# More seven-product steps in the early blocks of a hybrid decoder layer

## The chip, the cores and the metric

The kernel runs on one core of a Trainium2 chip. The metric is the device time of one execution in microseconds (us), lower is better. Before the change three runs gave 1722.56, 1724.4 and 1725.03 us; the median is 1724.4 us.

The engines of a core that matter here: TensorE multiplies (PE in the profile, its weight loads PEld), VectorE (DVE) and ScalarE (ACT) work elementwise, SyncE (SP) issues most DMA transfers. Each engine works through its own list of instructions in the order of the program, and waits on semaphores where another engine must be done first.

## What is computed

One layer of a decoder with two parallel branches, for 256 positions and 2048 channels in float32. The part that the change touches is the first large projection, `a @ W_in`, where `a` is the normalised input and `W_in` has 17408 columns that are shared out among attention, recurrence and gates:

```python
a = rmsnorm(h, norm_mix_pre[layer])
proj = a @ w_in[layer]
q_a, k_a, v_a, q_r, f_r, i_r, g_r, gate_a, gate_r = split_columns(proj)
...
y = jax.nn.sigmoid(gate_a) * (attn @ w_attn_branch[layer]) + jax.nn.sigmoid(gate_r) * (r_out @ w_hgrn_branch[layer])
h = h + rmsnorm(y @ w_mix_out[layer], norm_mix_post[layer])
a = rmsnorm(h, norm_ffn_pre[layer])
gt, up = jnp.split(a @ w_ffn_gate_up[layer], [D_FF], axis=-1)
ff = (jax.nn.silu(gt) * up) @ w_ffn_down[layer]
h = h + rmsnorm(ff, norm_ffn_post[layer])
```

## The kernel before

**Precision.** Every float32 operand is split into a rounded high part and a remainder, low = value - high. A product of two float32 tiles is three matmuls: high x high, high x low, low x high. The split of the weights is made on the chip as they stream in: ScalarE rounds (the high part), VectorE subtracts (the low part).

**Blocks and steps.** The program is a list of blocks, each a product of the activations with some columns of a weight matrix, and each block is a list of steps. The early stage of the kernel is two narrow blocks (1024 columns of the recurrence's output gate in all, line 1286), and then eight wide blocks of 1024 columns each: four for the two branch gates, three for the attention values, one for the recurrence's values (the list `early`, line 1289). After those come other stages, which the change leaves alone.

**A wide block** (class `Wide`) has eight steps. Step (m, s) takes the m-th 256 rows of the weights in two halves k = 0, 1 of 128 rows, and the block's two groups of 512 columns g = 0, 1: four weight tiles of 128 x 512. The activations are likewise two halves k by two sides of 128 positions. So a step is a 2 x 2 block product.

- s = 0, a **plain step**: eight products, 24 matmuls. Its split is one activation of 128 x 2048 (line 328) and one subtraction of 128 x 2048 (line 330).
- s = 1, a **seven-product step**: the scheme of Strassen in Winograd's form, seven products, 21 matmuls. Its split first forms sums of weight tiles on VectorE (line 334, 128 x 1024; lines 340 and 341, 128 x 512 each), rounds these on ScalarE (lines 339 and 342), rounds three of the plain tiles on ScalarE (line 345, `dh`), and subtracts for the low parts on VectorE (line 346, 128 x 2048, and line 348, 128 x 1536, `dl`). It needs four sums of activation tiles as well, made once for each m and kept in `x7[m]` (`pair_sums` and `seven_sums`, lines 400 to 422, lines 418, 405, 408 to 411 in the profile).

Of the seven products four go to banks of their own in PSUM (`p1`, `p5`, `p6`, `p7`); after the last seven-product step of a block `gather` (line 389) combines them in one activation and four additions. The outputs of a block are four more banks. `evac_kept` (line 662) ends a block: four additions (line 669), four activations (line 673) and four DMAs to DRAM that ScalarE issues (line 674). The roles of the two pools of four banks, `aux` and `acc`, are exchanged from one block to the next (`flip`).

**Order.** The order of work is written out by hand in the main loop (line 1343). At step n it does, in this order: the split of step n + 2 (`AHEAD` = 2), the load of the weights three further units on, the matmuls of step n, `gather` if this was the block's last seven-product step, some small work from side lanes, and at the end of a block its output. So the splits of the first two steps of a block are issued ahead of the output of the block before. The weight buffer `raw`, the high part `w` and the low part `wl` have three buffers each; the sums (`sum`), `dh` and `dl` of a seven-product step have one each.

**What the steps of the blocks are** stands in two lists (line 37 on). `FIRST`, for the first wide block, has plain steps alone. `EIGHT`, for the other seven (and for the blocks of the feed-forward part), has seven-product steps at its third, fifth and seventh place, with m = 0, 1, 2. The activation sums for `X7` = (0, 1, 2) are made beside the second narrow block, in a side lane (`more_x`, line 643).

Of the kernel before, what the change touches and what calls it, by code (L numbers as in the profile page):

```python
# [32 lines left out]
COL_QR, COL_FR, COL_IR, COL_GR = 9216, 10240, 11264, 12288  # L33
COL_GA, COL_GB = 13312, 15360

X7 = H7 = (0, 1, 2)
FIRST = [(m, 0) for m in range(8)]
EIGHT = [(3, 0), (4, 0), (0, 1), (5, 0), (1, 1), (6, 0), (2, 1), (7, 0)]
DOWN = [[(m, m in by7) for m in range(KF // 2)] for by7 in (range(4, 20, 3), range(3, 19, 3))]

# [50 lines left out]
def tile_hybrid_block(ctx: ExitStack, tc: tile.TileContext, t, out):  # L91
# [18 lines left out]
    def rslot(s):  # L110
        return rpool.tile([P, 1024], F32R, tag="r", bufs=16, name=nm(s))
# [107 lines left out]
    def add_seven(*args, flip, **kw):  # L219
        b = Wide(*args, **kw)  # L220
        b.flip = flip
        blocks.append(b)
        for i in range(b.steps):
            seq.append(Step(b, i, len(units), 0))
            units.append([seq[-1]])
# [187 lines left out]
    def pair_sums(x, which, store, slot):  # L413

        for m in which:
            f = ptile("f").rearrange("p (k t) -> p k t", k=2)
            xs = x.slots[m]
            nc.vector.tensor_add(f, xs[:, :, 0, :].bitcast(F32), xs[:, :, 1, :].bitcast(F32))
            dst = slot().rearrange("p (z n t) -> p z n t", z=2, n=4)
            yield  # L420
            seven_sums(f, dst)()
            store[m] = sums_of(dst)
            yield
# [127 lines left out]
    def flush(q):  # L551
        while q:
            advance(q)
# [6 lines left out]
    xT = Split("xT", KD)  # L560
# [80 lines left out]
    x7 = {}  # L641

    def more_x(c):
        if c + 2 < KD // 2:
            transpose_in(xt, colg, xT, c + 2)
        else:
            lanes[1].append(pair_sums(xT, X7[c - 6 :: 2], x7, lambda: rslot("so")))

# [13 lines left out]
    def evac_kept(key, fn):  # L662
        def go(b):
            dst = keep(key, 1024)
            for s, g in ((0, 0), (0, 1), (1, 0), (1, 1)):
                src = b.bank[s, g]
                if b.rest:
                    e = b.rest[s, g]
                    nc.vector.tensor_add(e, src, e)
                    src = e  # L670
                else:
                    e = eslot()
                nc.scalar.activation(e, src, fn, scale=r1c[:, s : s + 1])
                nc.scalar.dma_start(dst[:, s, g * 512 : (g + 1) * 512], e)
            yield
        return go
# [594 lines left out]
    w_in = t["w_in"][0]  # L1271
# [18 lines left out]
             (COL_GA + 1024, ("a", 1), AF.Sigmoid), (COL_GB + 1024, ("r", 1), AF.Sigmoid)]  # L1290
    early += [(COL_V + 1024 * g, ("v", g), AF.Copy) for g in range(3)] + [(COL_IR, "i", AF.Copy)]
    for n, (col, key, fn) in enumerate(early):
        add_seven(w_in, (col, col + 512), EIGHT if n else FIRST, xT, lambda m: x7[m],
                  evac_kept(key, fn), flip=n % 2 == 1, turn=1,
                  pre=(lambda: flush(lanes[1])) if n == 1 else None)
    for half in range(2):
# [141 lines left out]
```

## Time and profile before

| | |
|---|---|
| median of three runs | 1724.4 us |
| the profiled execution | 1723.16 us |
| its span, first to last instruction | 1721.4 us |
| granted TensorE clock, mean | 0.998 |
| first wide block on TensorE | 62.5 to 106.1 us |
| the seven other early wide blocks | 106.1 to 396.4 us |
| bytes moved by DMA | 344.78 MB |

How the profile is read: times are microseconds from the span's start. A line of the timeline has the start, the duration, the engine, the line of the program, the operation, the tile written and the tiles read, and in square brackets how long the engine had been idle before and which instruction of which engine ended that. A line of the chain has start, duration, engine, tile, line and the number of instructions. A line of a table by stretches has the length, then busy time and number of instructions for PE, PEld, DVE, ACT and POOL, then the granted clock, the busy share of the DMA engines and what they moved in GB/s.

### The profile page before, as it was taken

The numbers are of one execution on the slowest core, as the hardware profiler recorded it, in microseconds if no ns is written. First come the engines' busy times: TensorE is split into PE (matmuls) and PEld (weight loads), VectorE is DVE, ScalarE is ACT, GpSimd is POOL, SyncE is SP. The second block draws the span as 40 slices with busy tenths as digits, with TensorE's granted clock in tenths as the row PEclk, the third lists the DMA queues.
The fourth block names the chain that finished last, engine by engine and source line by source line (L and its number), as shares of the span: only waits on it lengthen the run. The fifth ranks groups of instructions, "written<-read, shape, count | busy, mean of one in ns | idle before, by whom it ended". The sixth has DMA issues, their size and how long they took to land.

```text
span 1721.4 us, 21535 instructions
## 1 busy us (share of the span) xinstructions
PE 1705.4 (99%) x8357; PEld 1431.0 (83%) x8357; DVE 1356.9 (79%) x1477; ACT 895.9 (52%) x1007; POOL 21.7 (1%) x38
## 2 busy tenths in 40 slices
PE   9999999999999999999999999999999999999997
PEld 7788888888888898888888877888888888888886
DVE  6668888886677887777666578888888888898998
ACT  6545555554435434544444465555555555665663
POOL 0000000000000000000000000000000000000000
PEclk9999999999999999999999999999999999999999
DMA  7765666667544645565556745555555555666653
GB/s 253 272 220 208 232 231 221 220 226 251 185 158 159 220 159 172 173 206 167 164 172 202 245 163 196 196 195 196 197 201 201 203 201 201 217 198 217 201 197 116
DMA packets 208742, 344.78 MB, mean 200 GB/s; under 512 B 10960, under 2 KB 77696, under 8 KB 208640
## 3 DMA queue, kind: packets, MB, share of 16 engines
q1 hardware_dynamic: 198848, 319.41, 55.1%
q10 hardware_dynamic: 6880, 13.51, 2.1%
q0 software_dynamic: 2912, 10.49, 1.8%
q8 instruction: 65, 1.06, 0.2%
q14 instruction: 37, 0.30, 0.1%
HBM read 331.83 MB, written 11.53 MB: 199 GB/s over the span
## 4 chain that ended last, share of the span: by engine, by line
PE 96%; DVE 1%; ACT 1%; DMA 1%; issue 0%; SPq 0%; DVEq 0%; ACTq 0%
PE acc L132 62%; PE aux L132 33%; PE aux L491 0%; DVE w L294 0%; PE aux L817 0%; DMA gpost<-in_norm_mix_post 0%; PE acc L1131 0%; DVE fz L1258 0%; ACT w L293 0%; PE aux L1131 0%; PE aux L479 0%; ACT junk L1212 0%; DVE e L1208 0%; ACT junk L1105 0%; DVE wl L330 0%
## 5 line engine op out<-in xcount | busy, mean ns | idle before, releaser
L294 DVE TENSOR_TENSOR w<-raw,w 128x1024 fp32r<-128x1024 f32 (+1 forms) x225 | 274.1, 1219 | 188.0 <-ACT w L293 187.2
L293 ACT ACTIVATE w<-raw 128x1024 fp32r<-128x1024 f32 (+1 forms) x225 | 237.1, 1055 | 289.1 <-PE acc L132 250.2
L132 PE MATMUL acc<-xT,w 128*128 128x256 f32 (+1 forms) x2048 | 370.4, 339 | 0.0
L132 PEld LDWEIGHTS acc<-xT,w 128*128 128x128 f32 x2048 | 311.6, 188 | 43.3
L330 DVE TENSOR_TENSOR wl<-raw,w 128x2048 fp32r<-128x2048 f32 x125 | 285.8, 2287 | 63.4 <-ACT w L328 63.3
L328 ACT ACTIVATE w<-raw 128x2048 fp32r<-128x2048 f32 x125 | 238.8, 1911 | 133.8 <-PE aux L132 66.7
L346 DVE TENSOR_TENSOR wl<-sum,w 128x2048 fp32r<-128x2048 f32 x63 | 144.3, 2291 | 65.0 <-ACT w L342 63.9
L132 PE MATMUL acc<-w,hT 128*128 128x512 f32 x622 | 182.5, 392 | 1.5 <-DVE w L294 1.2
L132 PE MATMUL acc<-w,xT 128*128 128x512 f32 x536 | 157.3, 395 | 2.7 <-DVE w L294 1.5
L339 ACT ACTIVATE w<-sum 128x1024 fp32r<-128x1024 f32 x63 | 67.0, 1064 | 172.1 <-DVE sum L334 161.8
L132 PEld LDWEIGHTS acc<-w,hT 128*128 128x128 f32 x622 | 115.8, 188 | 27.0 <-DVE w L294 2.5
L132 PE MATMUL aux<-w,hT 128*128 128x512 f32 x430 | 135.6, 389 | 0.0
L132 PEld LDWEIGHTS acc<-w,xT 128*128 128x128 f32 x536 | 100.6, 189 | 24.9 <-DVE w L294 2.6
L132 PE MATMUL aux<-w,xT 128*128 128x512 f32 x386 | 121.1, 389 | 0.0
L348 DVE TENSOR_TENSOR dl<-raw,dh 128x1536 fp32r<-128x1536 f32 x63 | 110.4, 1752 | 0.0
L132 PEld LDWEIGHTS aux<-w,hT 128*128 128x128 f32 x430 | 80.7, 188 | 16.7
L345 ACT ACTIVATE dh<-raw 128x1536 fp32r<-128x1536 f32 x63 | 92.9, 1474 | 0.0
L132 PE MATMUL acc<-w,yT 128*128 128x512 f32 x384 | 88.2, 390 | 0.3 <-DVE w L294 0.3
L132 PEld LDWEIGHTS aux<-w,xT 128*128 128x128 f32 x386 | 72.6, 188 | 15.1
L132 PEld LDWEIGHTS acc<-w,yT 128*128 128x128 f32 x384 | 71.8, 188 | 15.5 <-DVE w L294 0.7
L132 PE MATMUL aux<-w,a 128*128 128x512 f32 x268 | 83.7, 389 | 0.0
L132 PE MATMUL acc<-w,a 128*128 128x512 f32 x268 | 83.7, 389 | 0.0
(258 smaller groups left out, 2654.4 us busy)
## 6 DMA issues: line engine op xcount, KB each, us to landing
raw<-in_w_in SPq DMA_DIRECT2D x271, 512.0 KB, 4.7
raw<-in_w_ffn_gate_up SPq DMA_DIRECT2D x176, 512.0 KB, 4.4
raw<-in_w_ffn_down SPq DMA_DIRECT2D x88, 512.0 KB, 4.8
raw<-in_w_mix_out SPq DMA_DIRECT2D x32, 512.0 KB, 5.0
kept<-e ACTq DMA_DIRECT2D x32, 256.0 KB, 4.5
raw<-in_w_hgrn_branch SPq DMA_DIRECT2D x16, 512.0 KB, 4.6
raw<-in_w_attn_branch SPq DMA_DIRECT2D x16, 512.0 KB, 4.6
v<-kept POOLq DMA_DIRECT2D x8, 512.0 KB, 6.4
```

Source lines behind the costliest of these rows:

```text
L132: nc.tensor.matmul(ps, lhsT, rhs, start=start, stop=stop, skip_group_check=True)
L293: nc.scalar.activation(wh[:, k], raw[:, k], AF.Copy)
L294: nc.vector.tensor_sub(wl[:, k], raw[:, k], wh[:, k].bitcast(F32))
L328: nc.scalar.activation(hi, raw, AF.Copy)
L330: nc.vector.tensor_sub(lo, raw, hi.bitcast(F32))
L339: nc.scalar.activation(hi[:, :1024], s[:, :1024], AF.Copy)
L345: nc.scalar.activation(dhi, d, AF.Copy)
L346: nc.vector.tensor_sub(lo, s, hi.bitcast(F32))
L348: nc.vector.tensor_sub(dlo, d, dhi.bitcast(F32))
```

## The change

The first wide block takes three of its steps (m = 0, 2, 1, at the fifth, sixth and seventh place) by seven products. Every second later wide block of the early stage, that is the third, fifth and seventh, takes four steps (m = 0, 1, 2, 3, at the second, fourth, sixth and seventh place) by seven products instead of three. The other four, and the wide blocks of the feed-forward part, stay as they are. The activation sums are made for m = 3 too.

```diff
-X7 = H7 = (0, 1, 2)
-FIRST = [(m, 0) for m in range(8)]
+X7, H7 = (0, 1, 2, 3), (0, 1, 2)
+FIRST = [(3, 0), (4, 0), (5, 0), (6, 0), (0, 1), (2, 1), (1, 1), (7, 0)]
+FOUR = [(4, 0), (0, 1), (5, 0), (1, 1), (6, 0), (2, 1), (3, 1), (7, 0)]
 EIGHT = [(3, 0), (4, 0), (0, 1), (5, 0), (1, 1), (6, 0), (2, 1), (7, 0)]
...
     for n, (col, key, fn) in enumerate(early):
-        add_seven(w_in, (col, col + 512), EIGHT if n else FIRST, xT, lambda m: x7[m],
+        order = FIRST if n == 0 else EIGHT if n % 2 else FOUR
+        add_seven(w_in, (col, col + 512), order, xT, lambda m: x7[m],
                   evac_kept(key, fn), flip=n % 2 == 1, turn=1,
                   pre=(lambda: flush(lanes[1])) if n == 1 else None)
```

## The prediction

> **What bounds the kernel now.** I read the page first (span and the engines' busy time), then the chain in order of time for the early stage, then TensorE's waits there, then the order of VectorE and ScalarE inside one block.
>
> ```profile
> span 1721.4 us, 21535 instructions
> PE 1705.4 (99%) x8357; PEld 1431.0 (83%) x8357; DVE 1356.9 (79%) x1477; ACT 895.9 (52%) x1007; POOL 21.7 (1%) x38
> ```
> ```profile
> 62.47 43.59 PE aux L132 x191
> ...
> 147.54 12.24 PE aux L132 x54
> ...
> 189.02 12.24 PE acc L132 x54
> ```
> ```profile
> PE aux L132 <- DVE wl L330: 0.4, 1, 0.4
> ```
>
> TensorE, busy 99% of the span, sets the end. In the eight wide blocks of the early stage its only wait is 0.4 us. A run of 54 matmuls takes 12.24 us, so one costs 0.2267 us. A plain step has 24 (5.44 us), a seven-product step 21 (4.76 us). A block with three of the latter has 183 matmuls, 41.48 us, which is what lies between 147.54 and 189.02; the first, with none, has 192 and takes 43.59 us. That is the bound today. Whether it stays the bound depends on how far VectorE and ScalarE run ahead, and their rows show a thin lead. The block followed here has its first matmul at 230.34 us: 147.38 in the row below plus two blocks of 41.48.
>
> ```profile
> 147.38 0.39 PE L132 MATMUL aux<-w,xT 128*128 128x512 f32 x1
> ```
> ```profile
> 224.55 0.68 DVE L394 TENSOR_TENSOR e<-aux,e 128x512 f32<-128x512 f32 x1
> ...
> 227.34 2.28 DVE L330 TENSOR_TENSOR wl<-raw,w 128x2048 fp32r<-128x2048 f32 x1
> 229.53 2.48 DVE L669 TENSOR_TENSOR e<-acc,e 128x512 f32<-128x512 f32 x4
> 231.93 1.22 DVE L334 TENSOR_TENSOR sum<-raw 128x1024 f32<-128x1024 f32 x1
> ...
> 239.08 1.75 DVE L348 TENSOR_TENSOR dl<-raw,dh 128x1536 fp32r<-128x1536 f32 x1
> ...
> 242.95 1.22 DVE L334 TENSOR_TENSOR sum<-raw 128x1024 f32<-128x1024 f32 x1
> ...
> 246.76 2.29 DVE L346 TENSOR_TENSOR wl<-sum,w 128x2048 fp32r<-128x2048 f32 x1 [1.13 <-ACT w L342]
> 248.97 1.75 DVE L348 TENSOR_TENSOR dl<-raw,dh 128x1536 fp32r<-128x1536 f32 x1
> 250.63 2.29 DVE L330 TENSOR_TENSOR wl<-raw,w 128x2048 fp32r<-128x2048 f32 x1
> 252.84 1.22 DVE L334 TENSOR_TENSOR sum<-raw 128x1024 f32<-128x1024 f32 x1
> ```
>
> The reader is to see three prices on VectorE, start to start. A **seven split** takes 242.95 to 250.63 = 7.68 us, the 1.13 us of waiting for ScalarE's second rounding (L342) included, which every such split has. A **plain split** takes 2.21 us (250.63 to 252.84). Gather takes 2.79 us (224.55 to 227.34), the output's four adds 2.40 us (229.53 to 231.93). And the lead: the third step of this block starts its matmuls at 230.34 + 2 x 5.44 = 241.22; its last piece (L348) ends at 239.08 + 1.75 = 240.83. 0.39 us.
>
> So VectorE's bill for a block of today is 3 x 7.68 + 5 x 2.21 + 2.79 + 2.40 = 39.3 us, against TensorE's 41.48. A block of four costs 4 x 7.68 + 4 x 2.21 + 5.19 = 44.8 us, while TensorE falls to 180 x 0.2267 = 40.8. **The bound changes engine in every block of four.**
>
> **The change part by part.** 3 + 3 x 1 = 6 steps lose 3 matmuls each: 18 x 0.2267 = 4.08 us less on TensorE, 2.04 of it in the first block and 0.68 in each of the three blocks of four. Each such step adds 7.68 - 2.21 = 5.47 us on VectorE. What of it shows, I follow through the in-order queues, with ScalarE's rows beside them.
>
> ```profile
> 234.83 1.06 ACT L339 ACTIVATE w<-sum 128x1024 fp32r<-128x1024 f32 x1 [0.46 <-DVE sum L341]
> ...
> 238.12 1.91 ACT L328 ACTIVATE w<-raw 128x2048 fp32r<-128x2048 f32 x1
> ...
> 245.66 1.06 ACT L342 ACTIVATE w<-sum 128x1024 fp32r<-128x1024 f32 x1 [0.33 <-DVE sum L341]
> ```
>
> From the two lists: in a seven split that begins at s, L341 lets L342 start at s + 2.71, L346 starts at s + 3.81, L348 at s + 6.02 and ends at s + 7.77. After the output's adds begin, ScalarE is held 5.30 us (229.53 to 234.83) by four activations and their four DMA issues, before it can round anything for the next split. Splits are issued two steps ahead, so the split of a block's second step stands in both queues *ahead of* the output of the block before, and the split of its third step *behind* it. Today the second step is plain. In a block of four it is a seven. Times below count from the block's first matmul (0 = 230.34).
>
> *A block of four, third step.* Split of step 1 (counting from 0) begins where 227.34 stands: -3.00, and ends at +4.77; step 1 needs it at 5.44, fine. The adds begin at -3.00 + 7.68 = 4.68 instead of -0.81. ScalarE is free for step 2's rounding at 4.68 + 5.30 = 9.98; with L328's 1.91 it is done at 11.89; VectorE's L330 runs 11.93 to 14.22. Step 2 wants it at 5.44 + 4.76 = 10.20. A late second matmul restarts as this one did:
>
> ```profile
> 62.47 0.50 PE L132 MATMUL aux<-wl,xT 128*128 128x512 f32 x1 [0.39 <-DVE wl L330]
> 62.80 0.39 PE L132 MATMUL aux<-w,xT 128*128 128x512 f32 x1
> ```
>
> 0.06 us after the piece is there, 0.33 to the next matmul: at 14.28 and 14.61, against an undisturbed third matmul at 10.65. **3.96 us lost**; step 3 begins at 14.61 + 22 x 0.2267 = 19.60.
>
> *Its fourth step* (seven): split from 14.14, L348 ends at 21.91, wanted at 19.60: third matmul at 22.30 instead of 20.05, **2.25 us**; step 4 begins at 22.30 + 19 x 0.2267 = 26.61. *Steps 4 and 5*: plain split to 24.1, seven split 24.03 to 31.80, wanted at 26.61 and 32.05: nothing lost. *Step 6*, the seven that follows a seven: split from 31.71, L348 ends at 39.48, wanted at 32.05 + 4.76 = 36.81: third matmul at 39.87 instead of 37.26, **2.61 us**. Its dh has a single buffer and so waits for the ninth matmul of step 5 to end (8 x 0.2267 + 0.39 behind its first, 34.3), but L342 holds ScalarE to 31.71 + 2.71 + 1.06 = 35.5 anyway: that wait is hidden, and without this cover it would cost nothing until it passes 37. Step 7 and the two plain steps that open the next block have their splits done at 41.6, 43.8 and 48.8, wanted at 44.2, 49.6 and 55.1: the next block's adds begin 0.8 us before its first matmul, as today, so nothing is carried over. Sum of a block: 3.96 + 2.25 + 2.61 - 0.68 = **+8.1 us**, three times +24.4.
>
> *Loads.* SP issues a step's two 512 KB loads when the split three steps before has read its buffer, and that split is now up to some 8 us later.
>
> ```profile
> raw<-in_w_in SPq DMA_DIRECT2D x271, 512.0 KB, 4.7
> ```
>
> Step 5's buffer is free at 14.2 (step 2's L330), so its weights land near 20 and are first read at 24.0. The closest is step 1 of the next block: its buffer is free at 39.5, the weights land near 44.7 (a second issue behind the first, 0.5 us, and 4.7), and ScalarE would read them at 44.2. I take nothing; the 0.5 us would come off the next block's lead.
>
> *The first block*, and x7's fourth entry. The operand sums of pair 3 are a fourth round of L418, L405 to L411; the third round shows the price.
>
> ```profile
> 53.53 0.28 DVE L405 SCALAR_TENSOR_TENSOR s<-f 128x128 f32<-128x128 f32 x1
> ...
> 55.24 0.69 DVE L411 TENSOR_TENSOR so<-s,so 128x512 fp32r<-128x512 f32 x1 [0.70 <-ACT so L410]
> ...
> 60.12 4.50 DVE L330 TENSOR_TENSOR wl<-raw,w 128x2048 fp32r<-128x2048 f32 x2 [1.01 <-ACT w L328]
> ```
>
> L418 (the round's first operation) fits into the 1.01 us idle before 60.12. The rest goes between the two splits of 60.12: VectorE from 62.33 (60.12 + 2.21) to 64.74 by the first two rows, and ScalarE's rounding for the second split moves behind the sums' own, to 63.93 to 65.85. That L330 ends at 68.17. The step before it has its third matmul at 62.80 and so ends its turn at 62.80 + 22 x 0.2267 = 67.79: third matmul of the second step at 68.56, 0.32 us late. Behind this stand the gate's last operations on VectorE:
>
> ```profile
> 74.34 0.69 DVE L750 TENSOR_TENSOR g<-sig,gainr 128x512 f32<-128x512 f32 x1
> ```
>
> They end at 75.03 today and slip by something between 0 and the round trip's 2.4 us; I take 1.5. The three sevens in a row are then split from 76.5, 84.18 and 91.86, and ready at 84.27, 91.95 and 99.63. Step 4 starts at 68.56 + 22 x 0.2267 + 2 x 5.44 = 84.43 (fine), step 5 is wanted at 89.19 (its third matmul is 2.70 us late), step 6 at 96.65 (2.92 us). Sum: 0.32 + 2.70 + 2.92 - 2.04 = **+3.9 us**; -2.0 if all were hidden, +4.7 with the full slip.
>
> *The clock.* Stalls of TensorE may cost more than their length.
>
> ```profile
> 56.21 0.51 PE L132 MATMUL acc<-w,xT 128*128 128x512 f32 x1 [1.14 <-ACT w L293]
> 57.47 4.30 PE L132 MATMUL acc<-w,xT 128*128 128x512 f32 x11 [0.75 <-DVE w L294]
> ```
> ```profile
> 59.00:60.00 1.00, 1.00 (x4) 0.79 (x3) 0.11 (x1) 1.00 (x2) 0.00 (x0) 0.50 0.91 313
> ```
>
> After idle stretches of only 1.14 and 0.75 us the granted clock (the 0.50) was half, and the 11 matmuls from 57.47 took 4.30 us instead of 10 x 0.2267 + 0.5 = 2.77: 1.5 us. After the third-step stall, and after step 5 of the first block, such a slow stretch falls into time that the next stall would have lost anyway. After step 6 of the first block and of each block of four it would be paid in full: 4 x 1.5 = 6.0 us at most, 0 at least. One stall of 2.4 us idle is longer than those two together, but no row shows one of that length; I take the middle, two of four, 3.0 us.
>
> The Trainium skill ("TensorE: Matmul & The Clock Gate", Part 1) has the clock fall to half only after an idle window of about 3.4 us. The row above disagrees: it fell with a matmul between two gaps that sum to 1.9 us. By the page these stalls would leave the clock alone; that is the third rival below.
>
> Sum against the profiled execution (1723.16 us, span 1721.4, 1.8 us around it): 1723.2 + 24.4 + 3.9 + 3.0 = 1754.5. The three runs' median, 1724.4, is 1.2 us above that execution, so the forecast in their terms is **1755.7 us**.
>
> **The rivals.**
> (1) *The matmuls count and nothing else*: VectorE and ScalarE absorb the splits, -4.1 us, 1720.3, faster. It holds if step 2's rounding starts by 10.20 - 2.29 - 1.91, about 6 us into the block; so the output's adds must begin by 0.7, and their queue places them at 4.68. For it: TensorE alone waits for nothing today. Against: 39.3 of 41.48 us are taken already.
> (2) *Throughput only*: VectorE falls behind, but the queues' order costs nothing beyond that. Two blocks: 39.3 + 1.1 (the split of 231.93 takes 1.1 longer, its rounding standing behind the output's activations) and 44.8 + 1.1 make 86.3 against 82.96 today, +3.3 a pair, +10 in all with nothing for the first block: 1734.
> (3) *Stalls as worked out, clock full throughout*: 1724.4 + 24.4 + 3.9 = 1752.7.
> (4) *The blocks of three stall too*, since their lead is 0.39 us: late loads or the four clock drops push it under, one stall of about 1 us in each of four blocks, and the other two clock drops, 3.0: 1763.
> (5) *Nothing measurable*: gain and stalls cancel, 1724.4; only if most of the +28 is absent.
>
> **How the numbers follow.** Forecast (1753 to 1759) 0.42; (1) 0.08; (2) 0.14; (3) 0.23; (4) 0.10; (5) 0.03. The range goes from (2)'s 1734 to (4)'s 1764; it leaves out (1), (5) and the tails of (2) and (4). Within 0.2%, 3.4 us, a measurement of this kernel cannot tell a change from none; faster 0.08, same 0.03, slower 0.89.
>
> **What would show it.** In the changed trace: 8339 matmuls; TensorE waiting for L330 in the third step of each block of four (about 4 us), and for L348 in its fourth and seventh (2.3 and 2.7); blocks of four near 49.6 us, of three 41.5; the adds of L669 before a block of four about 4.7 us after its first matmul; granted clock of 0.5 to 0.8 in slices after the stalls. I am wrong if the adds stand ahead of the seven split on VectorE, or if the third step's L328 starts before 6 us.

## The result, and the profile after

Four runs of the changed kernel gave 1752.47 to 1756.81 us, median 1755.46; four runs of the kernel before in the same comparison have a median of 1724.38. The ratio is 1.0182, with a 95% interval of 1.017 to 1.0194: 31 us slower, where 4 us of matmuls were taken out. The forecast was 1755.7.

The page of the changed kernel, its span, the engines' busy time and the DMA total:

```profile
span 1754.2 us, 21557 instructions
...
PE 1715.1 (98%) x8339; PEld 1433.9 (82%) x8339; DVE 1389.6 (79%) x1515; ACT 905.8 (52%) x1021; POOL 21.6 (1%) x38
...
DMA packets 208742, 344.78 MB, mean 197 GB/s; under 512 B 10960, under 2 KB 77696, under 8 KB 208640
```

18 matmuls are gone (8357 to 8339), no byte more is moved, and VectorE is busy 32.7 us longer, the same 79% of a longer span. The page alone does not say where the time went; the chain of the early stage does. Start, duration, engine, tile and number of instructions of the stretches that open the blocks of three:

```profile
111.43 12.24 PE acc L133 x54
...
203.99 12.24 PE acc L133 x54
...
294.99 12.24 PE acc L133 x54
...
387.59 12.24 PE acc L133 x54
```

Before, the second wide block began at 106.06. It now begins at 111.43: 5.4 us lost in the first block. From one of these lines to the next lie a block of three (still 41.48 us) and a block of four, so the three blocks of four take 51.08, 49.52 and 51.12 us in place of 41.48 each: 9.6, 8.0 and 9.6 us. 5.4 + 27.3 = 32.7 of the 32.8 us by which the spans differ. Next to nothing was lost or won elsewhere.

TensorE's waits between 40 and 440 us (waiting engine, what for; total, times, longest):

```profile
PE aux L133 <- DVE dl L349: 10.1, 7, 2.1
PE aux L133 <- DVE wl L331: 7.3, 4, 1.8
PE aux L133 <- ACT w L329: 4.5, 3, 1.5
...
PE aux L133 <- ACT dh L346: 0.2, 1, 0.2
```

Where one wait of 0.4 us stood, TensorE now waits 22 us for the split, of both kinds: for the pieces of seven splits (`dl`), and for those of plain splits (`w`, `wl`) that stand behind them. One of the four waits for `wl`, 1.83 us, is the old one at the head of the first block and costs nothing: the matmul behind it starts at 62.75, and started at 62.80 before. (The lines of the functions named here are one higher than before.) This is what it looks like in one block of four, the one whose first matmul starts at 152.75. First VectorE's timeline:

```profile
149.75 1.22 DVE L335 TENSOR_TENSOR sum<-raw 128x1024 f32<-128x1024 f32 x1
...
157.43 2.48 DVE L670 TENSOR_TENSOR e<-acc,e 128x512 f32<-128x512 f32 x4
164.60 2.29 DVE L331 TENSOR_TENSOR wl<-raw,w 128x2048 fp32r<-128x2048 f32 x1 [4.70 <-ACT w L329]
...
172.81 1.75 DVE L349 TENSOR_TENSOR dl<-raw,dh 128x1536 fp32r<-128x1536 f32 x1
...
190.37 1.75 DVE L349 TENSOR_TENSOR dl<-raw,dh 128x1536 fp32r<-128x1536 f32 x1
```

Then ScalarE's, from the output of the block before to the late rounding:

```profile
158.14 0.72 ACT L674 ACTIVATE e<-e,r1c 128x512 f32<-128x512 f32 x1 [3.25 <-DVE e L670]
158.90 0.33 ACTq L675 DMA_DIRECT2D kept<-e  x1
...
162.66 1.91 ACT L329 ACTIVATE w<-raw 128x2048 fp32r<-128x2048 f32 x1 [0.40 <-ACT e L674]
```

And TensorE's at the third step (the first row is the last matmul of the second step):

```profile
162.72 0.39 PE L133 MATMUL aux<-w,xT 128*128 128x512 f32 x1
164.62 0.49 PE L133 MATMUL aux<-w,xT 128*128 128x512 f32 x1 [1.51 <-ACT w L329]
166.95 0.50 PE L133 MATMUL aux<-wl,xT 128*128 128x512 f32 x1 [1.83 <-DVE wl L331]
```

Read the three together. The seven split of the second step begins 3.00 us ahead of the block (149.75), the four adds of the output before stand behind it (157.43, that is 4.68 into the block), ScalarE issues four activations with their DMAs until 162.6, only then rounds the third step's weights, and VectorE, which has itself idled 4.70 us for that, ends at 166.89. TensorE's second matmul of the step starts 0.06 us later. TensorE waits for VectorE's subtraction, VectorE for ScalarE's rounding, ScalarE for its four activations of the output, and these for VectorE's adds, which stand behind the seven split; each engine keeps to its order.

### The profile page after: what moved, and what is told of

Its sections match the earlier page's. It is cut to its first block, busy times and chain, and to the rows that moved or that the text cites. A ratio compares the mean times of both kernels' runs of the same rounds, so it can differ in the third digit from the quotient of the medians.

```text
span 1754.2 us, 21557 instructions
## 1 busy us (share of the span) xinstructions
PE 1715.1 (98%) x8339; PEld 1433.9 (82%) x8339; DVE 1389.6 (79%) x1515; ACT 905.8 (52%) x1021; POOL 21.6 (1%) x38
## 3 DMA queue, kind: packets, MB, share of 16 engines
q8 instruction: 65, 1.06, 0.3%
## 4 chain that ended last, share of the span: by engine, by line
PE 86%; DVE 8%; ACT 3%; issue 2%; DMA 1%; ACTq 0%; SPq 0%; DVEq 0%
PE acc L133 58%; PE aux L133 26%; DVE dl L349 1%; DVE wl L347 1%; DVE sum L335 1%; ACT w L343 1%; ACT w L329 1%; DVE wl L331 1%; DVE sum L341 1%; DVE sum L342 1%; ACT e L674 1%; DVE w L295 0%; PE aux L818 0%; PE aux L492 0%; DMA gpost<-in_norm_mix_post 0%
## 5 line engine op out<-in xcount | busy, mean ns | idle before, releaser
L331 DVE TENSOR_TENSOR wl<-raw,w 128x2048 fp32r<-128x2048 f32 x119 | 271.8, 2287 | 57.3 <-ACT w L329 57.2
L329 ACT ACTIVATE w<-raw 128x2048 fp32r<-128x2048 f32 x119 | 226.6, 1908 | 98.7 <-PE aux L133 39.3
L347 DVE TENSOR_TENSOR wl<-sum,w 128x2048 fp32r<-128x2048 f32 x69 | 158.1, 2291 | 68.8 <-ACT w L343 65.4
L340 ACT ACTIVATE w<-sum 128x1024 fp32r<-128x1024 f32 x69 | 73.3, 1063 | 212.7 <-DVE sum L335 210.9
L349 DVE TENSOR_TENSOR dl<-raw,dh 128x1536 fp32r<-128x1536 f32 x69 | 120.9, 1752 | 0.0
L133 PE MATMUL aux<-w,xT 128*128 128x512 f32 x302 | 102.2, 409 | 4.5 <-ACT w L329 4.5
L346 ACT ACTIVATE dh<-raw 128x1536 fp32r<-128x1536 f32 x69 | 101.7, 1474 | 0.0
L335 DVE TENSOR_TENSOR sum<-raw 128x1024 f32<-128x1024 f32 x69 | 84.1, 1218 | 0.6 <-DMA raw<-in_w_ffn_down 0.6
L343 ACT ACTIVATE w<-sum 128x1024 fp32r<-128x1024 f32 x69 | 73.1, 1060 | 20.5 <-DVE sum L342 20.5
```

The source lines that it names most:

```text
L133: nc.tensor.matmul(ps, lhsT, rhs, start=start, stop=stop, skip_group_check=True)
L329: nc.scalar.activation(hi, raw, AF.Copy)
L331: nc.vector.tensor_sub(lo, raw, hi.bitcast(F32))
L335: nc.vector.tensor_sub(s[:, :1024].rearrange("p (a c) -> p a c", a=2), raw[:, 512:1536].rearrange("p (a c) -> p a c", a=2), raw[:, None, : ...
L340: nc.scalar.activation(hi[:, :1024], s[:, :1024], AF.Copy)
L343: nc.scalar.activation(hi[:, 1024:], s[:, 1024:], AF.Copy)
```

## The experiments

Eight kernels, in two batches; each is timed against the kernel before on the same chip.

**1. The blocks of four alone.**

```diff
-FIRST = [(3, 0), (4, 0), (5, 0), (6, 0), (0, 1), (2, 1), (1, 1), (7, 0)]
+FIRST = [(m, 0) for m in range(8)]
```

> The change with the first wide block put back to eight plain steps; the three blocks of four stay. Queue theory (the prediction's): each block of four takes 49.6 us on TensorE instead of 41.5, with its stalls at the third, fourth and seventh step, plus 1.5 us where a drop of the clock after the seventh step's stall is paid: +24.4 and up to 4.5, so 1749 to 1753, ratio 1.014 to 1.017. Throughput rival: VectorE's bill alone, +3.3 us for each pair of blocks, +10 in all, 1734, ratio 1.006. If the blocks of four only suffer because the first block hands them a late start, their length falls to 41 to 43 us and the time to 1724 to 1728.

1750.47 us against 1723.27, ratio 1.0158 (1.0143 to 1.0173): +27.2 us. Its blocks of four take 49.5, 49.5 and 51.4 us, worked out as above. The theory of the queues holds; throughput alone (+10) is out, and so is a late start inherited from the first block.

**2. The first block alone.**

```diff
-        order = FIRST if n == 0 else EIGHT if n % 2 else FOUR
+        order = EIGHT if n else FIRST
```

> The change with the three blocks of four put back to EIGHT; the first wide block keeps its three sevens in a row, and the activation sums are made for m = 3 too though nothing reads them. Queue theory: stalls of 2.7 and 2.9 us at the sixth and seventh step against 2.0 saved, +3.9, and 0 to 3 for the clock: 1727 to 1731, ratio 1.002 to 1.004; the following seven blocks 41.5 us each. Rival, all hidden: -2.0, 1722, ratio 0.999. If first block and blocks of four act on each other, this and the first run do not add up to the whole change (+31).

1727.01 us, ratio 1.0021 (1.0012 to 1.0031): +3.7 us. The seven blocks behind it are 41.48 us each, to the hundredth. The two parts add up: 27.2 + 3.7 = 30.9, against 31.1 for the whole. That is closer than the single runs allow, which spread over 2.2 us in either.

**3. The same four sevens at other places.**

```diff
-FOUR = [(4, 0), (0, 1), (5, 0), (1, 1), (6, 0), (2, 1), (3, 1), (7, 0)]
+FOUR = [(4, 0), (5, 0), (0, 1), (6, 0), (1, 1), (2, 1), (3, 1), (7, 0)]
```

> The change with the same four sevens in the blocks of four, but at the third, fifth, sixth and seventh place instead of the second, fourth, sixth and seventh; so the output of the block before stands ahead of the first seven split again, as in EIGHT. The work of every engine is the same as in the change. Queue theory: no stall at the third and fourth step, 2.2 us at the sixth, 2.9 at the seventh, less 0.7 saved: a block of four takes 45.9 us instead of 49.6, so 3 x 3.7 = 11 us less than the change: 1744, and 1740 to 1748 with the clock. Throughput rival: the same VectorE bill, so the same time as the change, 1755. Rival, the single dh buffer of neighbouring sevens is what costs: three neighbours instead of two, slower than the change, 1758 or more.

1743.93 us, ratio 1.0117 (1.0102 to 1.0132): +20.7 us, where the change has +31.1. The chain's stretches, as above:

```profile
109.43 12.24 PE acc L133 x54
...
196.78 12.24 PE acc L133 x54
```

87.35 - 41.48 = 45.87 us for a block of four; 45.9 was expected. No engine has less to do here than in the change, only the output of the block before is no longer behind a seven split. So not quite half of the loss in a block of four (3.7 of 8.1 us) is place, and what is left is VectorE's bill. That a third neighbour made it faster, not slower, also speaks against the single `dh` buffer. The page of the changed kernel agrees: ScalarE, which fills that buffer, was never idle ahead of this rounding (the last figure).

```profile
L346 ACT ACTIVATE dh<-raw 128x1536 fp32r<-128x1536 f32 x69 | 101.7, 1474 | 0.0
```

**4. The weight sums on GpSimd.**

```diff
-        s, d = p3("sum", F32, 2048, 1), raw[:, 512:]
-        nc.vector.tensor_sub(
+        s, d = p3("sum", F32, 2048, 2 if b.w is w_in else 1), raw[:, 512:]
+        sums = nc.gpsimd if b.w is w_in else nc.vector
+        sums.tensor_sub(
...
-        nc.vector.tensor_add(s[:, 1024:1536], raw[:, 512:1024], s[:, 512:1024])
-        nc.vector.tensor_sub(s[:, 1536:], raw[:, 1536:], s[:, 1024:1536])
+        sums.tensor_add(s[:, 1024:1536], raw[:, 512:1024], s[:, 512:1024])
+        sums.tensor_sub(s[:, 1536:], raw[:, 1536:], s[:, 1024:1536])
```

> The change with the three weight sums of a seven split (the 128x1024 subtraction and the two 128x512 operations) made by GpSimd instead of VectorE in the early stage, and two buffers for them there. VectorE's seven split falls from 7.68 to about 3.9 us and loses its wait for the second rounding, so its bill for a block of four falls from 44.8 to about 30 us. If VectorE's bill is the cause: the stalls at the fourth and seventh step go, TensorE sets the end again, and the 18 matmuls show: 1720 to 1725. GpSimd's own price is known only from 128x256 additions of 0.74 us; by that a split's sums take 5.9 us there, one at a time, which should be hidden. If GpSimd is slower than that, or slows VectorE's reads down, some stalls stay: 1730 to 1750. If the cause were the matmuls' order or the loads, nothing changes: 1755.

1770.59 us, ratio 1.0275 (1.0259 to 1.029): a miss, +47.3 us where the change has +31.1, and outside every range that was put down. GpSimd's timeline, a stretch of it:

```profile
210.93 1.29 POOL L343 TENSOR_TENSOR sum<-raw,sum 128x512 f32<-128x512 f32 x1
213.00 2.42 POOL L336 TENSOR_TENSOR sum<-raw 128x1024 f32<-128x1024 f32 x1 [0.78 <-DMA raw<-in_w_in]
215.50 3.22 POOL L342 TENSOR_TENSOR sum<-raw,sum 128x512 f32<-128x512 f32 x1
218.79 2.68 POOL L343 TENSOR_TENSOR sum<-raw,sum 128x512 f32<-128x512 f32 x1
```

and VectorE's in the same stretch:

```profile
217.49 2.84 DVE L350 TENSOR_TENSOR dl<-raw,dh 128x1536 fp32r<-128x1536 f32 x1
220.26 3.37 DVE L331 TENSOR_TENSOR wl<-raw,w 128x2048 fp32r<-128x2048 f32 x1
223.55 2.28 DVE L348 TENSOR_TENSOR wl<-sum,w 128x2048 fp32r<-128x2048 f32 x1
```

The two engines slow each other down. GpSimd's 128x512 operation takes 1.29 us alone and 3.22 beside VectorE's; VectorE's `dl` takes 2.84 instead of 1.75 and its 128x2048 subtraction 3.37 instead of 2.29 while GpSimd works, and 2.28 as soon as it has stopped. And VectorE waits longer. Its rows for the large subtraction between 100 and 400 us, the change first (count; busy time, mean ns of one; idle before, and what ended it):

```profile
L347 DVE TENSOR_TENSOR wl<-sum,w 128x2048 fp32r<-128x2048 f32 x22 | 50.4, 2293 | 29.4 <-ACT w L343 27.1 <-PE acc L133 2.3
...
L348 DVE TENSOR_TENSOR wl<-sum,w 128x2048 fp32r<-128x2048 f32 x22 | 60.1, 2733 | 72.5 <-ACT w L344 72.5
```

The three sums took VectorE 58.4 us there and are gone. But this subtraction and `dl` take 20.6 us more, and the wait for the second rounding, which now stands behind GpSimd's sums, grows from 27.1 to 72.5 us. The run therefore says nothing against VectorE's bill as the cause: it did not lower the bill as it was meant to.

**5. The pieces of a seven split in another order.** The operations are the same; `dl` comes ahead of `wl`, so that VectorE has something to do while ScalarE makes the second rounding. For this `dh` is rounded first, and it gets a second buffer.

```diff
+        early = b.w is w_in
         s, d = p3("sum", F32, 2048, 1), raw[:, 512:]
+        if early:
+            dhi, dlo = p3("dh", F32R, 1536, 2), p3("dl", F32R, 1536, 1)
+            nc.scalar.activation(dhi, d, AF.Copy)
...
         nc.scalar.activation(hi[:, 1024:], s[:, 1024:], AF.Copy)
         next(prep, None)
+        if early:
+            nc.vector.tensor_sub(dlo, d, dhi.bitcast(F32))
+            nc.vector.tensor_sub(lo, s, hi.bitcast(F32))
+            st.parts = hi, lo, dhi, dlo
+            return
```

> The change, and in the early stage the pieces of a seven split in another order: ScalarE rounds the plain tiles (dh, now two buffers) first, and VectorE makes dl before it makes wl, so that dl's 1.67 us cover the wait of 1.13 us for the second rounding of the sums. The operations are the same. VectorE's seven split should fall from 7.68 to about 6.5 us, its bill for a block of four from 44.8 to 40.2, and the piece that the second matmul needs is ready 2.2 us earlier. Queue theory: the stalls at the fourth and seventh step go; the one at the third step stays, since the output still stands behind a seven split there, 3.96 less 1.2 = 2.7 us; a block of four takes 43.5 us, 45 with a drop of the clock; the first block gains about 1: 1728 to 1735. Rival, VectorE's bill alone counts and its place in the order does not: all 18 matmuls show, 1720. Rival, the wait of 1.13 us is not the lever: 1750 to 1755.

1733.25 us, ratio 1.0059 (1.0046 to 1.0073): 21 of the 31 us are back, without one operation less. TensorE's waits between 60 and 440 us:

```profile
PE aux L133 <- DVE wl L331: 7.3, 4, 1.8
PE aux L133 <- ACT w L329: 0.9, 3, 0.3
PE aux L133 <- DVE dl L350: 0.6, 1, 0.6
```

The waits for `dl` have gone (10.1 to 0.6 us), those for `wl` stand as they were (7.3 us: three at the third step, and the one at the head of the first block). The blocks of four take 45.2, 45.1 and 43.5 us.

**6. The same, with the sevens where no output is late.**

```diff
-FIRST = [(3, 0), (4, 0), (5, 0), (6, 0), (0, 1), (2, 1), (1, 1), (7, 0)]
-FOUR = [(4, 0), (0, 1), (5, 0), (1, 1), (6, 0), (2, 1), (3, 1), (7, 0)]
+FIRST = [(3, 0), (4, 0), (5, 0), (0, 1), (2, 1), (6, 0), (1, 1), (7, 0)]
+FOUR = [(4, 0), (5, 0), (0, 1), (1, 1), (6, 0), (2, 1), (3, 1), (7, 0)]
```

> As the run before, and the same number of sevens put at places where no split stands behind a late output: the fourth, fifth and seventh place in the first block, and the third, fourth, sixth and seventh in the blocks of four. Queue theory: no stall in the early stage; a block of four takes 40.8 us, the first block 41.6 instead of 43.6, and the 18 matmuls show: -4.1 us, 1719 to 1721, ratio 0.9976. If a pair of neighbouring sevens costs of itself (dl has one buffer): +0.7 for each pair, 7 pairs, no gain, 1724. If the order of the splits was the smaller part and something else holds the blocks of four: over 1728.

1719.49 us against 1722.91, ratio 0.9978 (0.9969 to 0.9987): 3.4 us faster than the kernel before, and 34.5 us below the change, by the two differences, with the same number of sevens. Its chain around a block of four:

```profile
146.04 12.24 PE aux L133 x54
...
186.84 12.24 PE acc L133 x54
```

40.80 us, which is 180 x 0.2267: TensorE is the bound again, and the sevens show.

**7. The new order on the kernel before.** The edit of run 5 alone, with the old lists.

> The kernel before with the new order of the pieces of a seven split alone (three sevens a block, none in the first). TensorE is the bound there, so the 1.13 us that VectorE wins at each split should show nowhere: 1723 to 1725, ratio 1.000; the lead of the third step's dl grows from 0.4 to about 3 us. If the lead of 0.4 us was costing something unseen: up to 1 us less.

1723.62 us, ratio 1.0001 (0.9991 to 1.001). The order of the pieces is worth nothing where TensorE is the bound. The gain of run 6 is that of the matmuls.

**8. Four sevens in all seven later blocks.**

```diff
-        order = FIRST if n == 0 else EIGHT if n % 2 else FOUR
+        order = FOUR if n else FIRST
```

> As the second run of this batch, but all seven later blocks of the early stage take four sevens (at the third, fourth, sixth and seventh place). 30 matmuls fewer than before: -6.8 us if all of it shows, 1717. VectorE's bill is 40.2 us for a block, and some 41.2 with the first split of a block behind the output's activations, against 40.8 on TensorE, so it falls behind by up to 0.4 us a block, which the lead of about 3 us at the third step should carry over seven blocks: 1717 to 1719. If the lead is used up by the second block in a row: 1722 to 1728.

On top of run 6. 1725.48 us, ratio 1.0012 (1.0003 to 1.0021): a miss, 6 us slower than run 6 where 2.7 us faster was expected. It lies in the range (1722 to 1728) that was put down for a lead used up early. VectorE's adds that end two blocks, one behind the other, and the wait between them:

```profile
147.32 2.48 DVE L679 TENSOR_TENSOR e<-acc,e 128x512 f32<-128x512 f32 x4
...
154.07 1.76 DVE L350 TENSOR_TENSOR dl<-raw,dh 128x1536 fp32r<-128x1536 f32 x1 [1.69 <-ACT dh L338]
...
189.40 2.48 DVE L679 TENSOR_TENSOR e<-aux,e 128x512 f32<-128x512 f32 x4
```

A block takes 42.08 us on VectorE, not 41.2: the first `dl` of a block waits 1.69 us for a `dh` that stands behind the four activations and DMA issues of the output, which I had put at about 1. At 42.08 against 40.80, VectorE falls behind by 1.3 us a block. TensorE's timeline shows from when on this counts:

```profile
204.78 0.50 PE L133 MATMUL acc<-dl,xT 128*128 128x512 f32 x1 [0.54 <-DVE dl L350]
...
246.85 0.50 PE L133 MATMUL aux<-dl,xT 128*128 128x512 f32 x1 [0.51 <-DVE dl L350]
```

The lead carries the first of the seven blocks and most of the second. In the third TensorE waits for `dl`, and so in each behind it (the later ones at 288.93, 331.01 and 373.09, again some 42.08 us apart): five blocks go at VectorE's pace, 6.4 us in all. With the blocks of three in between (run 6) VectorE catches up.

## Why the prediction was right

**The bound changes engine: right.** VectorE's bill was put at 44.8 us against 40.8 for a block of four. Run 3 leaves the bill as it is and moves only the order, and what stays, 45.87 us a block, is the 44.8 plus the 1.1 us for which the first seven split waits behind the output's activations (rival 2's term). VectorE's timeline of that run has this wait, 2.26 us in place of 1.12 or 1.13, and between the adds of two outputs no other wait but one of 1.12 us in each of the other three seven splits:

```profile
157.28 2.29 DVE L347 TENSOR_TENSOR wl<-sum,w 128x2048 fp32r<-128x2048 f32 x1 [2.26 <-ACT w L343]
```

In run 5 a seven split takes 6.46 us in place of 7.68 (160.67 to 167.13), and the stalls for `dl` go. As that run also has `dl` ready ahead of `wl` and gives `dh` a second buffer, it does not part the length of the split from its order. Run 8 does: with the new order in every block, TensorE goes at VectorE's 42.08 us and not at its own 40.80.

**The stalls of a block of four, step by step: right.** Counted from the first matmul, with the prediction beside: adds at 4.68 (4.68), the third step's L331 starts at 11.85 (11.93), the fourth step's `dl` ends at 21.81 (21.91), the seventh's at 39.37 (39.48). The lead is back at the next block, since the blocks of three are still 41.48 us. The single `dh` buffer was hidden, as argued: TensorE waits for `dh` 0.2 us in all. So were the loads, which were taken as nothing: no wait of TensorE, VectorE or ScalarE between 108 and 430 us is ended by one.

**The first block: right, with the clock on top.** +3.9 was worked out without the clock, and the run with that block alone gave +3.7. The profiled execution of that run shows why this is less than the 5.4 of the change: there the clock dropped behind the first of the two stalls (the row below), the second wait was 1.03 us in place of 2.13, and so nothing was paid for the drop. In the change it came behind the second.

```profile
92.00:94.00 2.00, 2.00 (x6) 1.63 (x5) 1.65 (x3) 1.31 (x2) 0.00 (x0) 0.50 0.84 265
```

The stall of 0.3 us that was put down to the extra activation sums does not show: it fell into a slow stretch of the clock, which stood at 58 to 62 us before and stands at 62 to 66 us after, with a granted clock of 0.55 to 0.6 in both. Their slip does show. The gate's last operations, taken to end 1.5 us later, end 1.4 us later (76.46 in place of 75.03 us), and the three seven splits start behind them. (The full slip of 2.4 us would have made +4.8, not +4.7.)

**The clock: right in kind, one drop short.** This is the term that was mis-sized: two drops of 1.5 us were taken, and the profiled execution shows three that are paid. After the last stall of the first block, and after the seventh step of the three blocks of four, two rows each, the stretch with the stall and the one behind it (the third figure from the end of each line is the granted clock):

```profile
96.48:99.89 3.41, 1.06 (x4) 0.49 (x4) 3.41 (x3) 3.41 (x3) 0.00 (x0) 1.00 0.00 0
99.89:103.30 3.41, 3.41 (x10) 2.65 (x9) 3.41 (x2) 0.79 (x2) 0.00 (x0) 0.50 0.78 267
...
188.63:192.05 3.42, 1.43 (x6) 0.69 (x4) 3.42 (x3) 3.42 (x3) 0.00 (x0) 1.00 0.01 5
192.05:195.46 3.41, 3.29 (x8) 2.62 (x9) 3.41 (x3) 1.05 (x1) 0.00 (x0) 0.50 0.66 209
...
280.79:284.21 3.42, 1.82 (x8) 1.03 (x6) 3.42 (x2) 3.42 (x3) 0.00 (x0) 1.00 0.15 52
284.21:287.62 3.41, 2.90 (x13) 2.40 (x14) 3.41 (x3) 2.05 (x2) 0.00 (x0) 1.00 0.49 162
...
372.96:376.37 3.41, 1.41 (x7) 0.85 (x6) 3.41 (x3) 3.41 (x3) 0.00 (x0) 1.00 0.00 0
376.37:379.78 3.41, 3.41 (x10) 2.64 (x9) 3.41 (x2) 0.88 (x2) 0.00 (x0) 0.50 0.79 282
```

The same stall drops the clock twice and leaves it alone once, and that is the whole difference between the blocks of 51.1 and the one of 49.5 us; by the lengths of their blocks run 1 has one drop in three, and run 5 two in three, after the third-step stall that is left there. With this goes a wider spread of the times, 4.3 us for the changed kernel and 2.5 for the kernel before. The drops after the third-step stall were paid by the next stall, as the prediction had it: in the block shown, the fourth step's wait for `dl` shrank from 2.25 to some 0.3 us.

What tells the stalls that drop the clock from the one that does not is not their length, 2.11 and 2.00 us against 2.11 at the three seventh steps, but how they fall on a fixed beat. In each of the ten traces the stretches of half clock between 50 and 440 us last 3.41 us or twice that, and lie a whole number of 3.41 us apart. Cut on this beat, as the rows above are, the intervals ahead of the three drops have TensorE busy for 1.06, 1.43 and 1.41 us, the one without a drop for 1.82. Over the ten traces, every interval at full clock that was busy for less than 45% was followed by a drop, and none that was busy for more than half; in the few between, both occur. The rule of the Trainium skill ("TensorE: Matmul & The Clock Gate", Part 1) is an idle window of about 3.4 us, which runs freely: the length and the beat agree with these traces, but the window need not be idle.

So the prediction's "two of four" was a choice where it had no row to go by, and part of the closeness of the forecast is luck: its sum of the parts is 31.3 us, and the two profiled executions differ by 32.8, one drop more.

**The rivals.** Matmuls alone (1720) fell with the result, and came true in run 6 once both causes were taken out. Throughput alone (1734) fell with runs 1 and 3. Stalls with the clock full (1752.7) would do for the fastest run (1752.47), but not for the profiled one, which shows the drops. Stalls in the blocks of three did not occur.

## What to carry to other kernels

Before work is taken off the engine that sets the end, add up the in-order time of every engine that feeds it over one period, waits included that every period has. Where another engine's sum passes what the period takes today (here 44.8 us against 41.48), the change loses time, and here 31 us were lost where 4 were to be saved. Then look at what a longer piece now stands ahead of in its queue: with a look-ahead of two steps, the output of the last block was behind it, and with the first two sevens one place later a block of four lost little more than half as much. A wait that sits inside every piece can often be covered by an order of the same operations, which brought 21 of 31 us back, and with the sevens at better places let the matmuls count.

## What was not expected of the hardware

GpSimd is no spare engine beside a VectorE that subtracts. Its two-input operation went from 1.29 to 3.22 us and VectorE's from 2.29 to 3.37 while both read SBUF (run 4). The Trainium skill says this ("SBUF — State Buffer", "Who interferes with whom"): a VectorE instruction with two inputs in SBUF contends with a GpSimd instruction that reads SBUF. The rows agree, and the expectation of that run had left it open. They show turns: the ends of the two engines' rows alternate (GpSimd's at 218.72, VectorE's at 220.33, GpSimd's at 221.47, VectorE's at 223.63), each behind the other's by nearly what the operation takes alone (1.61 for 1.75, 1.14 for 1.29, 2.16 for 2.29 us).
